# Mixture-of-experts layer in fp32: the further slots' work under the conditional, row additions on VectorE, and the last expert's second product by column halves

## The chip, the cores and the metric

One core of a Trainium2 chip runs the whole program. The time is device microseconds from the start to the end of one execution. The kernel before takes 2110.71 us in the median of three runs (2107.49 to 2116.29).

## The reference

512 tokens of 1024 columns pass two layers. Each layer has a mixer of four branches (sliding-window attention, a recurrent branch, two further attentions), and then a feed-forward block: dense in the first layer, a mixture of eight experts in the second, two experts for each token. Everything is fp32. What the change touches is the end of the second layer:

```python
# D_MODEL 1024, D_FF_EXPERT 1408, 8 experts, top 2 of them for each of 512 tokens
h = silu(x @ exp_w1[e]) * (x @ exp_w3[e])     # [tokens of e, 1408]
y = h @ exp_w2[e]                             # [tokens of e, 1024]
out = layer_norm(DN_ALPHA * x + sum over the token's two experts of weight * y)
```

## The kernel before, in words

**Precision.** A weight piece of 128 x 1024 fp32 comes in by a DMA from SyncE (SP). ScalarE casts it to a rounded 32-bit form (whi, L1152), VectorE subtracts that from the original (wlo, L1153), and TensorE multiplies three times: high by high, high by low, low by high. So each piece costs a ScalarE cast, a VectorE subtraction and twelve or six matmuls in sequence.

**An expert.** Its first 128 tokens are its slots; up to 32 more are its *further* slots. Tokens that chose it are gathered, transposed, and multiplied: `up` does three chunks of columns (512, 512, 384), `turn` transposes the gated product of a chunk (`turn_main` for the 128 slots, the rest of `turn` for the further ones: transposes at L1466, a copy and SiLU on ScalarE at L1471 and L1474, an addition and a product on VectorE at L1472 and L1475), and `down` multiplies by the second matrix, eleven pieces. The order is written out: rows of the next expert are turned and its first chunk is multiplied before this one's `down` begins. A scheduler then sets each engine's order from it; marked lines (`high_priority`) go earlier.

**Further slots.** Their matmuls use the raw fp32 pieces with 32 columns of stationary data, four side by side, and stand under a conditional on the number of tokens of the expert (`further`, L1443): six conditionals in `up` and three in `down`. All engines come past each conditional. In the program before only TensorE has work in them. The buffer po is set to zero by VectorE first (L1404, L1486), so that what comes behind can run whether the block was taken or not: ScalarE copies po to go (L1438) or yo (L1523), and `down_more` adds up four groups by a matmul with a fixed matrix (L1529), VectorE copies (L1531) and GpSimd stores the rows (L1534) to Y in device memory. A token's row in Y is found by its slot number.

**The end.** Rows of experts 0 to 6 are gathered from Y token by token (`ask_rows`, GpSimd's indirect DMA, L1317, two for each block of 128 tokens, eight in all, into four buffers). `take_rows` multiplies each by its weight on ScalarE (L1706) and adds it to x on GpSimd in halves (L1709). The last expert's result isn't stored: `last` splits it, brings it to token order by matmuls with one-hot matrices (L1743 to L1746), adds it to x on VectorE (L1748), and the layer norm follows on VectorE with help of ScalarE and GpSimd.

Of the kernel before, what the change touches and what calls it, by code (L numbers as in the profile page):

```python
# [56 lines left out]
class Net:  # L57
# [1340 lines left out]
    def up(self, e, c, begin=None):  # L1398

        nc, I = self.nc, self.I  # L1400
        mm = nc.tensor.matmul
        n = min(512, FE - c * 512)
        pa, pb, po = self.triple()
        nc.vector.memset(po, 0.0)  # L1404
        r = 32 * (e % 4)
        xh, xl = self.xe[:, e % 2, 0], self.xe[:, e % 2, 1]
        late = []
        for k0 in range(0, KB, 2):
            raws = []
# [29 lines left out]
        return g, go, c, n  # L1439

# [16 lines left out]
    def turn(self, st):  # L1457

        nc = self.nc
        g, go, c, n = st  # L1460
        nb = n // P
        gt, gto = self.gT
        self.turn_main(g, c, n, gt)
        pt = self.ps("y")
# [4 lines left out]
        t = self.rf.tile([P, 4, 64], F32, name="sgo", tag="sgo", bufs=2)[:, 0:nb]  # L1469
        with self.tc.high_priority():  # L1470
            nc.scalar.copy(t, p4[:, :, 0])  # L1471
            nc.vector.tensor_add(t, t, p4[:, :, 1])  # L1472
            s = t[:, :, 0:32]
            nc.scalar.activation(s, s, AF.Silu)  # L1474
            nc.vector.tensor_mul(gto[:, c * 4:c * 4 + nb], s, t[:, :, 32:64])  # L1475

# [3 lines left out]

    def down(self, e, gT):
        nc, I = self.nc, self.I
        mm = nc.tensor.matmul
        gt, gto = gT
        p0, p1, po = self.triple()
        nc.vector.memset(po, 0.0)  # L1486
        late = []
        for f0 in range(0, EB, 2):
            if e == NE - 1 and f0 in (2, 6):
                self.take_rows(f0 // 4 + 1)  # L1490
                self.ask_rows(f0 // 4 + 2)
            fs = range(f0, min(EB, f0 + 2))
            raws = []
            for f in fs:
# [4 lines left out]
                for hf, ps in enumerate((p0, p1)):  # L1499
# [3 lines left out]
                    mm(ps, gt[:, 1, f], a, start=False, stop=f == EB - 1)  # L1503
                raws.append(raw)
            late += list(zip(fs, raws))
# [8 lines left out]
        if e == NE - 1:  # L1514
            self.take_rows(TB - 1)
            return p0, p1, po
        y = self.rf.tile([P, D], F32, name="yr", tag="yr", bufs=2)
        yo = self.rf.tile([P, 512], F32, name="yo", tag="yo", bufs=1)
# [5 lines left out]
        return yo  # L1524

    def down_more(self, e, yo):
# [6 lines left out]
        for hf in range(2):  # L1533
            nc.gpsimd.dma_start(self.Y[r:r + 32, hf * 512:(hf + 1) * 512], ys[32 * hf:32 * hf + 32])  # L1534

    def rest(self, dp):
# [127 lines left out]
    def slots(self):  # L1664
# [25 lines left out]

        z = mp.tile([P, D], F32, name="zero", tag="xg", bufs=2)
        nc.vector.memset(z[0:1], 0.0)
        nc.gpsimd.dma_start(self.Y[(NE - 1) * NS:(NE - 1) * NS + 1, :], z[0:1])

# [7 lines left out]
    def take_rows(self, *tbs):  # L1702
        for tb in tbs:
            for j in range(2):
                rows = self.yg[:, tb % 2 * 2 + j]
                self.nc.scalar.mul(rows, rows, self.wt[:, tb, j:j + 1])  # L1706
                for half in range(2):
                    xs = self.x[tb][half]
                    self.nc.gpsimd.tensor_add(xs, xs, rows[:, half * 512:(half + 1) * 512])  # L1709

    def last_begin(self):

        nc, mp = self.nc, self.rf
        num = self.num_t
        ido = mp.tile([P, 2], F32, name="ido")
        nc.vector.memset(ido, -1.0)
        for h in range(2):
            for i in range(2):
                r = 32 * (2 * i + h)
                nc.vector.tensor_copy(ido[r:r + 32, h:h + 1], self.own[96:128, 9:10])  # L1720
        self.ohl = []
        for n, col in enumerate((self.own[:, NE - 1:NE], ido[:, 0:1], ido[:, 1:2])):
# [4 lines left out]
    def last(self, pss, g, b):  # L1727

        nc, mp = self.nc, self.rf
        mm = nc.tensor.matmul  # L1730
        hl = []
        for n, ps in enumerate(pss):
            t = mp.tile([P, 2, 512], F32R, name="yl", tag="xg" if n == 2 else "yr", bufs=2)
            nc.scalar.copy(t[:, 0], ps)  # L1734
            nc.vector.tensor_sub(t[:, 1], ps, t[:, 0].bitcast(F32))
            hl.append(t)
        tags = ("r", "y", "s", "t", "o", "mm", "mm", "mm")
        for tb in range(TB):
            ts = slice(tb * P, (tb + 1) * P)
            for half in range(2):  # L1740
                ps = self.ps(tags[tb * 2 + half])
                a, o = self.ohl[0][:, ts], self.ohl[1 + half][:, ts]
                mm(ps, a, hl[half][:, 0], start=True, stop=False)  # L1743
                mm(ps, a, hl[half][:, 1], start=False, stop=False)
                mm(ps, o, hl[2][:, 0], start=False, stop=False)
                mm(ps, o, hl[2][:, 1], start=False, stop=True)  # L1746
                xs = self.x[tb][half]
                nc.vector.scalar_tensor_tensor(xs, ps, self.cw[:, tb, NE - 1:NE], xs, op0=OP.mult, op1=OP.add)  # L1748
                self.stats(tb, half)
            self.layer_norm(tb, g, b, spread=True)  # L1750
            self.store_x(tb, self.out)

    def moe(self, dp):
# [9 lines left out]
        self.new_gT()  # L1763
        self.links = {}
        self.preload(PRE)
# [11 lines left out]
        for e in range(NE):  # L1777
            gT = self.gT
            self.turn(st)
            if e > 0:  # L1780
                self.down_more(e - 1, yo)
            if e + 1 < NE:
# [3 lines left out]
            for c in (1, 2):  # L1786
                st = self.up(e, c)
                if c == 1:
                    self.turn(st)
                    self.tokens(e + 2)  # L1790
                    if e == 0:
                        self.dispatch(range(4, 8))
                    if e == 1:
                        self.wt, self.cw = self.weights("")
# [7 lines left out]
            self.turn(last)  # L1802
            if e == NE - 1:
                self.take_rows(0)
                self.ask_rows(1)
                self.last_begin()
            yo = self.down(e, gT)
        self.last(yo, g, b)

# [44 lines left out]
```

## Time and profile before

| | |
|---|---|
| runs | 2110.71 us median (2107.49 to 2116.29) |
| profiled execution | 2107.6 us, span 2105.9 us |
| TensorE (PE) | 96% busy, mean granted clock 0.988 |
| VectorE (DVE) | 65% |
| ScalarE (ACT) | 44% |
| GpSimd (POOL) | 7% (151.1 us) |
| experts of the second layer | from about 1580 us on |

The page gives busy time by engine, the span in slices, the chain that ended last, and groups of instructions by line. Other views of the same trace give windows (busy time of each engine in a stretch), timelines (one engine's instructions in order, with the idle time before them in brackets and what ended it), and waits. Starts are microseconds from the start of the span. `x2` folds two instructions in sequence into one row, whose duration is then that of both.

### The profile page before, as it was taken

The page shows a single profiled execution, that of the slowest core. Times are in us where ns is not written, and L with a number is a line of the kernel's source. Part 1 is how long each engine was busy: PE and PEld are TensorE (multiplying, and loading weights), DVE is VectorE, ACT ScalarE, POOL GpSimd, SP SyncE. Part 2 cuts the span into 40 slices and gives each one's busy share as a digit, 9 for nine tenths or more (in the row PEclk, how much of TensorE's full clock was granted, in tenths as well). Part 3 has the DMA queues.
Part 4 walks back from the last instruction along what each step waited for, and adds up shares of the span by engine and source line. Part 5 has one row for each costly group of instructions (what it writes and reads, how often), then busy time and mean ns, then how long its engine had stood idle before and what let it go on. Part 6 is the DMA issues. An engine that isn't in the chain of part 4 may idle for free. (4 is left out here: it accounts for less than half of the span.)

```text
span 2105.9 us, 31148 instructions
## 1 busy us (share of the span) xinstructions
PE 2019.7 (96%) x11240; PEld 1569.9 (75%) x11240; DVE 1366.6 (65%) x2732; ACT 918.0 (44%) x1561; POOL 151.1 (7%) x211
## 2 busy tenths in 40 slices
PE   8999999999999999999999999999989999999994
PEld 7767777778888888888767778768877766677663
DVE  5677779844563333236676769844568877788778
ACT  3354543333232222113464553332326666677663
POOL 1020200000000000000011200000000000000043
PEclk9999999999999999999999999999999999999997
DMA  5231213343343334233221213313538988898872
GB/s 159 69 84 39 57 41 90 90 125 96 94 146 99 101 93 133 92 98 115 77 58 43 70 41 90 90 51 95 176 128 308 352 291 304 295 342 306 293 280 82
DMA packets 274976, 294.56 MB, mean 140 GB/s; under 512 B 23852, under 2 KB 203416, under 8 KB 274808
## 3 DMA queue, kind: packets, MB, share of 16 engines
q1 hardware_dynamic: 267736, 273.90, 40.2%
q0 software_dynamic: 7072, 18.49, 2.8%
q8 instruction: 97, 1.59, 0.3%
q14 instruction: 71, 0.58, 0.1%
HBM read 276.74 MB, written 15.60 MB: 139 GB/s over the span
## 5 line engine op out<-in xcount | busy, mean ns | idle before, releaser
L98 ACT CAST whi<-wraw 128x1024 fp32r<-128x1024 f32 (+1 forms) x218 | 228.1, 1046 | 625.4 <-PE ps_mm L112 376.9
L99 DVE TENSOR_TENSOR wlo<-wraw,whi 128x1024 fp32r<-128x1024 f32 (+1 forms) x218 | 265.5, 1218 | 361.2 <-ACT whi L98 355.0
L113 PE MATMUL ps_mm<-xh,wlo 128*128 128x512 f32 (+1 forms) x1288 | 494.9, 384 | 3.1 <-DVE rs L259 3.1
L111 PE MATMUL ps_mm<-xh,whi 128*128 128x512 f32 (+1 forms) x1288 | 496.5, 386 | 0.6 <-ACT whi L98 0.5
L112 PE MATMUL ps_mm<-xl,whi 128*128 128x512 f32 (+1 forms) x1288 | 492.1, 382 | 0.3 <-DVE xl L233 0.3
L113 PEld LDWEIGHTS ps_mm<-xh,wlo 128*128 128x128 f32 x1288 | 243.7, 189 | 49.8 <-DVE wlo L99 3.4
L111 PEld LDWEIGHTS ps_mm<-xh,whi 128*128 128x128 f32 x1288 | 243.8, 190 | 46.5 <-issue 2.6
L112 PEld LDWEIGHTS ps_mm<-xl,whi 128*128 128x128 f32 x1288 | 243.7, 189 | 45.8 <-issue 2.3
L1153 DVE TENSOR_TENSOR wlo<-mwraw,whi 128x1024 fp32r<-128x1024 f32 (+1 forms) x98 | 124.2, 1282 | 17.2 <-ACT whi L1152 16.0
L1152 ACT CAST whi<-mwraw 128x1024 fp32r<-128x1024 f32 (+1 forms) x98 | 95.9, 1005 | 16.0 <-PE ps_t L1503 10.1
L470 ACT COPY bt_pt<-ps_t 128x512 f32<-128x512 f32 (+2 forms) x80 | 41.7, 522 | 85.4 <-PE ps_t L467 84.6
L1153 DVE TENSOR_TENSOR mwlo<-mwraw,mwhi 128x1024 fp32r<-128x1024 f32 (+1 forms) x62 | 71.9, 1175 | 6.9 <-ACT mwhi L1152 6.4
L451 ACT ACTIVATE bt_pt<-ps_s,mx 128x256 f32<-128x256 f32 (+3 forms) x128 | 61.8, 487 | 21.8 <-DVE mx L445 18.0
L260 POOL TENSOR_TENSOR rs<-rs,mhalf 128x1 f32<-128x1 f32 x16 | 13.8, 861 | 724.2 <-DVE rs L259 724.2
L442 DVE TENSOR_REDUCE mx<-ps_s 128x2 f32<-128x512 f32 (+3 forms) x80 | 48.5, 607 | 22.1 <-PE ps_s L406 21.1
L1152 ACT CAST mwhi<-mwraw 128x1024 fp32r<-128x1024 f32 (+1 forms) x62 | 61.0, 999 | 3.2 <-DMA mwraw<-in_exp_w_dram 2.3
L1114 DVE TENSOR_TENSOR bt_pt<-bt_pt,ps_mm 128x512 f32<-128x512 f32 x22 | 15.1, 688 | 70.4 <-PE ps_mm L113 63.0
L467 PE MATMUL ps_t<-ident,bt_pt 128*128 128x128 f32 x272 | 51.5, 283 | 6.0 <-DVE bt_pt L461 4.8
L609 DVE MAX8 m<-bt_pt 128x8 f32<-128x256 f32 (+2 forms) x96 | 53.8, 560 | 2.7
L1153 DVE TENSOR_TENSOR wlo<-ring,whi 128x1024 fp32r<-128x1024 f32 (+1 forms) x45 | 51.5, 1160 | 2.5 <-DMA mwraw<-in_exp_w_dram 1.2
L610 DVE MATCH_REPLACE8 bt_pt<-m,bt_pt 128x256 f32<-128x256 f32 (+2 forms) x96 | 52.1, 543 | 0.0
L111 PE MATMUL ps_mm<-bt_o,whi 128*128 128x512 f32 x128 | 51.2, 400 | 0.4 <-ACT bt_o L511 0.4
(710 smaller groups left out, 4119.1 us busy)
## 6 DMA issues: line engine op xcount, KB each, us to landing
mwraw<-in_exp_w_dram SPq DMA_DIRECT2D x124, 512.0 KB
wraw<-in_w_in_dram SPq DMA_DIRECT2D x106, 512.0 KB
wraw<-in_ffn_w_dram SPq DMA_DIRECT2D x66, 512.0 KB
ring<-in_exp_w_dram SPq DMA_DIRECT2D x60, 512.0 KB
wraw<-in_exp_w_dram SPq DMA_DIRECT2D x32, 512.0 KB
mwraw<-in_exp_w_dram SPq DMA_DIRECT2D x36, 384.0 KB
wraw<-in_w_branch_dram SPq DMA_DIRECT2D x20, 512.0 KB
wraw<-in_w_out_dram SPq DMA_DIRECT2D x16, 512.0 KB
```

The costliest lines, as they stand in the source:

```text
L98: nc.scalar.copy(h, src)
L99: (low or nc.vector).tensor_sub(l, src, h.bitcast(F32))
L111: mm(ps, wh, xh, start=start, stop=False)
L112: mm(ps, wh, xl, start=False, stop=False)
L113: mm(ps, wl, xh, start=False, stop=stop)
L442: nc.vector.tensor_reduce(mx[:, 0:nh], s3, op=OP.max, axis=AX.X)
L451: nc.scalar.activation(p3[:, h], s3[:, h], AF.Exp, bias=nm[:, h:h + 1], scale=0.125, accum_out=mx[:, 4 + h:5 + h])
L467: nc.tensor.transpose(pt[:, i * P:(i + 1) * P], p3[:, h, kb * P:(kb + 1) * P], self.ident)
L609: nc.vector.max(m8, sc[:, :nk])
L610: nc.vector.match_replace(sc[:, :nk], m8, sc[:, :nk], REPL)
L1152: self.chain("hi", lambda: nc.scalar.copy(hi[:, :n], src))
L1153: self.chain("lo", lambda: nc.vector.tensor_sub(lo[:, :n], src, hi[:, :n].bitcast(F32)))
```

## The change

Five things are done together.

1. The transposes of the further slots, their ScalarE and VectorE work, the copy of po and the fold of `down` move into the conditionals (`turn_more`, `down_more`). po isn't cleared any more but in the last expert. The first rows of Y for further slots, 225 of them, are set to zero once, while the first expert runs (`empty`: a GpSimd memset and two stores).
2. `take_rows` is 16 fused multiply-adds on VectorE in the place of 8 ScalarE products and 16 GpSimd additions.
3. The last expert's second product runs over the left 512 output columns first and then over the right ones (`down_last`), six pieces each: five of 128 x 1024 that hold two steps of 512 columns, and one of 128 x 512. There are three conditionals in each half.
4. `last` is called for each half. The further slots' sum is one tile for the half, so that four tiles are split, not three; matmuls of the fold are 32 as before.
5. One one-hot matrix serves the further slots, not two.

```diff
@@ up
-        nc.vector.memset(po, 0.0)
...
                 with self.further(e):
+                    if late[0][0] == 0 and c > 0:
+                        self.turn_more(c - 1)
                     for kk, raws in late:
...
+                    if k0 == KB - 2:
+                        go = self.go[c] = self.rf.tile([P, 512], F32, name="go", tag="go", bufs=2)
+                        nc.scalar.copy(go[:, :n], po[:, :n])
...
-            go = self.rf.tile([P, 512], F32, name="go", tag="go", bufs=2)
-            nc.scalar.copy(go[:, :n], po[:, :n])
@@ down
-        nc.vector.memset(po, 0.0)
...
                 with self.further(e):
+                    if late[0][0] == 0:
+                        self.turn_more(2)
                     for f, w in late:
...
+                    if late[-1][0] == EB - 1:
+                        self.down_more(e, po)
...
-            nc.scalar.copy(yo, po)
+    def down_more(self, e, po):
+        nc = self.nc
+        yo = self.rf.tile([P, 512], F32, name="yo", tag="yo", bufs=1)
+        nc.scalar.copy(yo, po)
         ps = self.ps("y")
         nc.tensor.matmul(ps[0:64], self.ident64, yo, start=True, stop=True)
...
+    def down_last(self, g, b):
...
+        for half in range(2):
+            cs = slice(half * 512, half * 512 + 512)
+            ps, po = [self.ps(t) for t in (("s", "t"), ("o", "mm"))[half]]
+            nc.vector.memset(po, 0.0)
+            late = []
+            for f0 in range(0, EB, 2):
+                if half == 0 and f0 in (2, 6, 10):
+                    self.take_rows(f0 // 4 + 1)
+                    if f0 < 10:
+                        self.ask_rows(f0 // 4 + 2)
+                m = min(2, EB - f0)
+                raw = self.moe_raw()[:, :m * 512]
...
+                for i in range(m):
+                    f = f0 + i
+                    wh, wl = h[:, i * 512:(i + 1) * 512], l[:, i * 512:(i + 1) * 512]
+                    self.chain("mm", lambda: mm(ps, gt[:, 0, f], wh, start=f == 0, stop=False))
+                    mm(ps, gt[:, 0, f], wl, start=False, stop=False)
+                    mm(ps, gt[:, 1, f], wh, start=False, stop=f == EB - 1)
+                    late.append((f, raw[:, i * 512:(i + 1) * 512]))
+                if len(late) >= 2 * HOLD or f0 + 2 >= EB:
+                    with self.further(e):
+                        if half == 0 and late[0][0] == 0:
+                            self.turn_more(2)
+                        for f, w in late:
+                            q = 32 * (f % 4)
+                            mm(po[q:q + 32], gto[:, f], w, start=f < 4, stop=f >= EB - 4, skip_group_check=True)
+                    late = []
+            self.last(half, ps, po, g, b)
@@ take_rows
-                self.nc.scalar.mul(rows, rows, self.wt[:, tb, j:j + 1])
                 for half in range(2):
                     xs = self.x[tb][half]
-                    self.nc.gpsimd.tensor_add(xs, xs, rows[:, half * 512:(half + 1) * 512])
+                    self.nc.vector.scalar_tensor_tensor(xs, rows[:, half * 512:(half + 1) * 512],
+                                                        self.wt[:, tb, j:j + 1], xs, op0=OP.mult, op1=OP.add)
```

The instructions' order on two engines shows where the moved work stands now. First TensorE, at the last conditional of `down` of expert 6. `gt` is the transposed product, `gto` that of the further slots, `ring`, `wraw` and `mwraw` are raw pieces, `whi`/`wlo` and `mwhi`/`mwlo` split ones. Before:

```order
L1507 COMPARE_AND_BRANCH
L1511 MATMUL ps_mm<-ring,gto 32x512 x4
L1511 MATMUL ps_mm<-wraw,gto 32x512 x2
L1507 UNCONDITIONAL_BRANCH x2
L1501 MATMUL ps_mm<-mwhi,gt 128x512 x2
L1502 MATMUL ps_mm<-mwlo,gt 128x512
L1503 MATMUL ps_mm<-mwhi,gt 128x512
L1502 MATMUL ps_mm<-mwlo,gt 128x512
L1503 MATMUL ps_mm<-mwhi,gt 128x512
L1501 MATMUL ps_mm<-whi,gt 128x512 x2
L1529 MATMUL ps_y<-yo,ident_110 64x512
L1502 MATMUL ps_mm<-wlo,gt 128x512
```

And of the change:

```order
L1506 COMPARE_AND_BRANCH
L1512 MATMUL ps_mm<-ring,gto 32x512 x4
L1512 MATMUL ps_mm<-wraw,gto 32x512 x2
L1528 MATMUL ps_y<-yo,ident_110 64x512
L1506 UNCONDITIONAL_BRANCH x2
L1501 MATMUL ps_mm<-mwhi,gt 128x512 x2
L1502 MATMUL ps_mm<-mwlo,gt 128x512
L1503 MATMUL ps_mm<-mwhi,gt 128x512
L1502 MATMUL ps_mm<-mwlo,gt 128x512
L1503 MATMUL ps_mm<-mwhi,gt 128x512
L1501 MATMUL ps_mm<-whi,gt 128x512 x2
L1502 MATMUL ps_mm<-wlo,gt 128x512
```

The fold of the further slots (L1529, now L1528) has moved from between the dense matmuls to the end of the block, ahead of them.

The second place is VectorE from the last subtractions to the first folding instruction. Before (`yl` is the last expert's split result, `bt_x` are the rows of x):

```order
L1153 TENSOR_TENSOR mwlo<-wraw,mwhi 128x1024 x2
L1153 TENSOR_TENSOR wlo<-mwraw,whi 128x1024
L1507 REGISTER_ALU x2
L1507 COMPARE_AND_BRANCH
L1507 UNCONDITIONAL_BRANCH x2
L1153 TENSOR_TENSOR wlo<-mwraw,whi 128x1024 x2
L1735 TENSOR_TENSOR yl<-ps_o,yl 128x512
L1735 TENSOR_TENSOR yl<-ps_s,yl 128x512
L1735 TENSOR_TENSOR yl<-ps_t,yl 128x512
L1748 SCALAR_TENSOR_TENSOR bt_x<-ps_r,cw,bt_x 128x512
```

And of the change, from the first product's last conditional to the second's first:

```order
L1751 SCALAR_TENSOR_TENSOR bt_x<-ring,wt,bt_x 128x512
L1153 TENSOR_TENSOR mwlo<-wraw,mwhi 128x1024
L1751 SCALAR_TENSOR_TENSOR bt_x<-ring,wt,bt_x 128x512
L1153 TENSOR_TENSOR wlo<-mwraw,whi 128x1024
L1751 SCALAR_TENSOR_TENSOR bt_x<-ring,wt,bt_x 128x512
L1153 TENSOR_TENSOR wlo<-mwraw,whi 128x1024 x2
L1153 TENSOR_TENSOR mwlo<-mwraw,mwhi 128x512
L1751 SCALAR_TENSOR_TENSOR bt_x<-ring,wt,bt_x 128x512 x9
L1776 TENSOR_TENSOR yl<-ps_s,yl 128x512
L1776 TENSOR_TENSOR yl<-ps_t,yl 128x512
L1543 MEMSET ps_mm 128x512
L1776 TENSOR_TENSOR yl<-ps_o,yl 128x512
```

Three fused additions stand between the last subtractions and nine in a row behind them; the subtractions of the first half's sums come only after those, and behind them the conditionals of the second half and the folds of both halves.

## Rows read from the trace of the kernel before

**Rows 1.** The page's busy table: busy us, share of the span, instructions.
```profile
PE 2019.7 (96%) x11240; PEld 1569.9 (75%) x11240; DVE 1366.6 (65%) x2732; ACT 918.0 (44%) x1561; POOL 151.1 (7%) x211
```

**Rows 2.** Windows: us, busy us by engine, TensorE's clock, DMA share, GB/s.
```profile
1640.00:2020.00 380.00, 374.70 (x1900) 265.63 (x1899) 300.68 (x345) 253.77 (x338) 15.93 (x24) 1.00 0.86 303
...
1842.90:1897.50 54.60, 53.13 (x244) 40.90 (x243) 48.02 (x56) 40.54 (x55) 3.17 (x5) 1.00 0.95 340
...
2034.00:2046.30 12.30, 9.22 (x43) 7.94 (x41) 10.70 (x11) 9.68 (x15) 9.45 (x7) 0.86 1.04 409
...
2058.00:2064.00 6.00, 0.62 (x2) 0.00 (x0) 6.00 (x1) 2.00 (x2) 6.00 (x6) 0.50 0.25 83
```

**Rows 3.** Timelines of the end: start, us, engine, line, [idle before <- releaser].
```profile
2033.70 1.15 ACT L1706 ACTIVATE ring<-ring,wt 128x1024 f32<-128x1024 f32 x1 [2.73 <-DMA ring<-Y,slot_i]
...
2052.25 4.07 DVE L1153 TENSOR_TENSOR wlo<-mwraw,whi 128x1024 fp32r<-128x1024 f32 x1
...
2056.81 9.95 DVE L1153 TENSOR_TENSOR wlo<-mwraw,whi 128x1024 fp32r<-128x1024 f32 x2
...
2057.18 7.37 POOL L1709 TENSOR_TENSOR bt_x<-bt_x,ring 128x512 f32<-128x512 f32 x6
...
2065.69 0.79 PE L1502 MATMUL ps_s<-wlo,gt 128*128 128x512 f32 x1 [7.07 <-DVE wlo L1153]
...
2071.93 1.23 DVE L1153 TENSOR_TENSOR wlo<-mwraw,whi 128x1024 fp32r<-128x1024 f32 x1 [0.62 <-ACT whi L1152]
...
2080.53 0.75 DVE L1748 SCALAR_TENSOR_TENSOR bt_x<-ps_r,cw,bt_x 128x512 f32<-128x512 f32 x1 [0.78 <-PE ps_r L1746]
```

**Rows 4.** Waits in the experts' stretch: waiter <- awaited: us, times, longest.
```profile
ACT go L1438 <- PE ps_o L1429: 20.0, 5, 4.7
...
ACT yo L1523 <- PE ps_mm L1511: 9.3, 3, 5.8
...
PEld ps_mm L1501 <- issue: 6.7, 10, 0.8
...
PEld ps_mm L1502 <- DVE wlo L1153: 5.7, 7, 0.8
```

**Rows 5.** TensorE's timeline at transposes of further slots in a skipped expert (3 and 2 of them).
```profile
1864.10 0.40 PE L1416 MATMUL ps_s<-whi,xe 128*128 128x512 f32 x1
...
1864.90 0.39 PE L1418 MATMUL ps_s<-whi,xe 128*128 128x512 f32 x1
...
1875.26 0.39 PE L1416 MATMUL ps_t<-mwhi,xe 128*128 128x512 f32 x1
1875.49 0.38 PE L1466 MATMUL ps_y<-ident,go 128*128 128x128 f32 x2
...
1875.94 0.39 PE L1418 MATMUL ps_t<-mwhi,xe 128*128 128x512 f32 x1
```

**Rows 6.** TensorE's timeline at the fold of a skipped expert.
```profile
1893.43 0.63 PE L1501 MATMUL ps_mm<-whi,gt 128*128 128x512 f32 x2
1894.00 1.07 PE L1529 MATMUL ps_y<-yo,ident 128*64 128x512 f32 x2
1895.00 0.50 PE L1502 MATMUL ps_mm<-wlo,gt 128*128 128x512 f32 x1
```

**Rows 7.** Timelines of TensorE and ScalarE behind a taken block of expert 6.
```profile
2014.54 0.73 PE L1501 MATMUL ps_mm<-mwhi,gt 128*128 128x512 f32 x2
...
2014.66 0.59 ACT L1523 COPY yo<-ps_mm 128x512 f32<-128x512 f32 x1 [5.82 <-PE ps_mm L1511]
```

**Rows 8.** Single lines: count, ns min/median/max, first and last start; a DMA's landing.
```profile
L274 DVE SCALAR_TENSOR_TENSOR bt_pt<-bt_pt,rs,bt_v x16: 740/746/751, 578.8 to 966.8; 128x512 f32<-128x512 f32 x16
...
L1152 ACT CAST whi<-mwraw x98: 816/1050/1073, 1574.8 to 2070.8; 128x1024 fp32r<-128x1024 f32 x77, 128x768 fp32r<-128x768 f32 x21
...
L1404 DVE MEMSET ps_o<- x15: 485/485/485, 1581.0 to 1992.7; 128x512 f32 x15
...
DMA to landing us min/median/max: 4.9/6.7/8.1
```

More of the change, by code (lines that the diff above doesn't have):

```diff
@@ L1457, in turn, with turn_more @@
     def turn(self, st):
+        g, c, n = st
+        self.turn_main(g, c, n, self.gT[0])
+    def turn_more(self, c):
         nc = self.nc
-        g, go, c, n = st
+        go, gto = self.go[c], self.gT[1]
+        n = min(512, FE - c * 512)
         nb = n // P
-        gt, gto = self.gT
-        self.turn_main(g, c, n, gt)
         pt = self.ps("y")
@@ L1469, in turn @@
         t = self.rf.tile([P, 4, 64], F32, name="sgo", tag="sgo", bufs=2)[:, 0:nb]
[L1470 to L1475, printed above, removed]
+        nc.scalar.copy(t, p4[:, :, 0])
+        nc.vector.tensor_add(t, t, p4[:, :, 1])
+        s = t[:, :, 0:32]
+        nc.scalar.activation(s, s, AF.Silu)
+        nc.vector.tensor_mul(gto[:, c * 4:c * 4 + nb], s, t[:, :, 32:64])
     def new_gT(self):
@@ L1479, in new_gT, with down @@
                    self.rf.tile([P, EB, 32], F32, name="gto"))
-    def down(self, e, gT):
+    def down(self, e):
         nc, I = self.nc, self.I
         mm = nc.tensor.matmul
-        gt, gto = gT
+        gt, gto = self.gT
         p0, p1, po = self.triple()
-        nc.vector.memset(po, 0.0)
         late = []
         for f0 in range(0, EB, 2):
-            if e == NE - 1 and f0 in (2, 6):
-                self.take_rows(f0 // 4 + 1)
-                self.ask_rows(f0 // 4 + 2)
             fs = range(f0, min(EB, f0 + 2))
-            raws = []
             for f in fs:
@@ L1503, in down @@
                     mm(ps, gt[:, 1, f], a, start=False, stop=f == EB - 1)
-                raws.append(raw)
-            late += list(zip(fs, raws))
+                late.append((f, raw))
             if len(late) >= 2 * HOLD or f0 + 2 >= EB:
                 with self.further(e):
+                    if late[0][0] == 0:
+                        self.turn_more(2)
                     for f, w in late:
@@ L1534, in down_more @@
             nc.gpsimd.dma_start(self.Y[r:r + 32, hf * 512:(hf + 1) * 512], ys[32 * hf:32 * hf + 32])
+    def down_last(self, g, b):
+        nc, I, e = self.nc, self.I, NE - 1
+        mm = nc.tensor.matmul
+        gt, gto = self.gT
+        for half in range(2):
[10 more added lines that the diff above has]
+                raw = self.moe_raw()[:, :m * 512]
+                with self.tc.high_priority():
+                    self.chain("load", lambda: nc.sync.dma_start(
+                        raw.rearrange("p (k c) -> p k c", k=m),
+                        I["exp_w2"][0, e, f0 * P:(f0 + m) * P, cs].rearrange("(k p) c -> p k c", p=P)))
+                h, l = self.moe_split(raw)
+                for i in range(m):
[14 more added lines that the diff above has]
+            self.last(half, ps, po, g, b)
     def rest(self, dp):
@@ L1689, in slots, with empty @@
         nc.vector.tensor_copy(self.slot, sf)
-        z = mp.tile([P, D], F32, name="zero", tag="xg", bufs=2)
-        nc.vector.memset(z[0:1], 0.0)
-        nc.gpsimd.dma_start(self.Y[(NE - 1) * NS:(NE - 1) * NS + 1, :], z[0:1])
+    def empty(self):
+        z = self.rf.tile([P, D], F32, name="zero", tag="yr", bufs=2)
+        self.nc.gpsimd.memset(z, 0.0)
+        n = (NE - 1) * (NS - P) + 1
+        for r in range(0, n, P):
+            m = min(P, n - r)
+            self.nc.gpsimd.dma_start(self.Y[(NE - 1) * P + r:(NE - 1) * P + r + m, :], z[0:m])
     def ask_rows(self, *tbs):
@@ L1714, in last_begin @@
         num = self.num_t
[L1715 to L1720, printed above, removed]
+        ido = mp.tile([P, 1], F32, name="ido")
+        for i in range(4):
+            nc.vector.tensor_copy(ido[32 * i:32 * i + 32], self.own[96:128, 9:10])
         self.ohl = []
-        for n, col in enumerate((self.own[:, NE - 1:NE], ido[:, 0:1], ido[:, 1:2])):
+        for n, col in enumerate((self.own[:, NE - 1:NE], ido)):
             t = mp.tile([P, T], F32R, name="ohl", tag="g", bufs=3)
@@ L1725, in last_begin, with last @@
             self.ohl.append(t)
-    def last(self, pss, g, b):
+    def last(self, half, ps, po, g, b):
         nc, mp = self.nc, self.rf
@@ L1731, in last @@
         hl = []
[L1732 to L1735, printed above, removed]
+        for n, src in enumerate((ps, po)):
+            t = mp.tile([P, 2, 512], F32R, name="yl", tag=("yr", "xg")[n], bufs=2)
+            nc.scalar.copy(t[:, 0], src)
+            nc.vector.tensor_sub(t[:, 1], src, t[:, 0].bitcast(F32))
             hl.append(t)
-        tags = ("r", "y", "s", "t", "o", "mm", "mm", "mm")
         for tb in range(TB):
             ts = slice(tb * P, (tb + 1) * P)
[L1740 to L1751, printed above, removed]
+            out = self.ps((("r", "y", "mm", "mm"), ("r", "y", "s", "t"))[half][tb])
+            for n in range(2):
+                for i in range(2):
+                    mm(out, self.ohl[n][:, ts], hl[n][:, i], start=n == 0 and i == 0, stop=n == 1 and i == 1)
+            xs = self.x[tb][half]
+            nc.vector.scalar_tensor_tensor(xs, out, self.cw[:, tb, NE - 1:NE], xs, op0=OP.mult, op1=OP.add)
+            self.stats(tb, half)
+            if half:
+                self.layer_norm(tb, g, b, spread=True)
+                self.store_x(tb, self.out)
     def moe(self, dp):
@@ L1802, in moe @@
             self.turn(last)
-            if e == NE - 1:
+            if e + 1 < NE:
+                self.down(e)
+            else:
                 self.take_rows(0)
@@ L1806, in moe @@
                 self.last_begin()
-            yo = self.down(e, gT)
-        self.last(yo, g, b)
+                self.down_last(g, b)
 def build(tc, I, out, taps=None, stage=99):
```

14 lines of the change are left out of this document (3 added, 11 removed).

## The prediction

> **What bounds the kernel now.** I read the page's busy table first, then the windows of the mixture-of-experts stretch, then the timelines of TensorE, VectorE and GpSimd at the places that the change edits. TensorE is busy 96% of the span [rows 1], and while the experts run it is 374.70 of 380 us, at full clock; VectorE beside it is 300.68 [rows 2]. So in that stretch time is saved by taking work off TensorE, and lost by making TensorE wait. The end is another matter. From 2046 on TensorE waits for VectorE, whose subtractions are stretched, and from 2080.53 VectorE alone does the last layer norm [rows 3]. The profiled run took 2107.6 us, 1.7 more than its span; the median of the three runs is 2110.71, 3.1 above it. I sum against the profiled run and add the 3.1 at the end. Half a per cent, about 10.6 us, is what a measurement of this kernel can tell from no change.
>
> **Skipped experts: the transposes and the fold.** Eight experts, of which the wait of ScalarE for L1511 shows three that take the conditional block (three waits, [rows 4]); five skip it. Today TensorE transposes the further slots of all eight. In a skipped expert one pair of transposes moves the second matmul behind it from an expected 1875.26 + 2 x 0.23 = 1875.72 to 1875.94, so 0.22 us, and the group of three in the last chunk from 1864.56 to 1864.90, 0.34 us [rows 5]. Eleven transposes are four pairs and one three: 4 x 0.22 + 0.34 = 1.2 us. The fold of the further slots (two fp32 passes, L1529) stands between a pair that starts at 1893.43 and a matmul at 1895.00, which would be due at 1893.90 [rows 6]: 1.1 us, in which a wait for VectorE may hide, so 0.6 to 1.1. Experts 0, 2, 4 and 5 save both, 4 x 2.3 = 9.2; the last one, which has no such fold, saves 1.2. Together **10.4 us** (8.4 at the lower price of the fold). The conditionals themselves stay: nine for each expert, at some two thirds of a microsecond of TensorE each (L1501's weight loads idled 6.7 us at ten of them with no other wait, [rows 4]); the last expert's three new ones fall where TensorE waits for VectorE anyway.
>
> **Taken experts: a new wait.** The fold now stands inside the conditional, behind the last small matmul and ahead of the dense ones (first order piece of the change). Before, TensorE went on with dense matmuls at 2014.54 while ScalarE copied yo from 2014.66 for 0.59 us [rows 7]. Now TensorE must sit through that copy, about 0.75 us with the handover, and VectorE copies ys before it leaves. Behind ScalarE in its queue stand the casts of the next weight pieces, and behind VectorE their subtractions; TensorE has one split piece in hand, six matmuls of 0.23 us and two more that need only the cast, 1.9 us, against a cast and a subtraction that end about as late. So about 1.0 us at this block. The three transposing blocks of such an expert send ScalarE and VectorE into the block with TensorE too, but there 16 small matmuls follow the transposes and cover the copy and the product; I take 0.4 for the three together. Three experts: 3 x 1.4 = **4.2 us lost**, from 2.3 (the yo copy alone) upwards; the upper end is the slower rival below.
>
> **Relief of VectorE.** The memsets of 0.485 us, 15 of them in one row of L1404 [rows 8] and 32 in all, shrink to two, and the small additions and products of skipped experts go. TensorE's weight loads waited 5.7 us in seven waits for a subtraction at L1502 alone [rows 4], but all of TensorE's idle time from 1640 to 2020 is 380 - 374.70 = 5.3 us [rows 2]. So the gain lies between 0 and 5; as most of that idle time stands at conditionals I take **1.5**.
>
> **The last expert and the row additions.** Beside GpSimd's six additions (7.37 us), two subtractions took 9.95 us, where an undisturbed one takes 1.23, and one before them 4.07 [rows 3]. That is 7.5 + 2.8 = 10.3 us, and TensorE waited 7.07 for it. It wasn't the loads: from 2058 to 2064 the DMA engines were busy a quarter of the time [rows 2]. With the additions off GpSimd these 10.3 us go. The Trainium skill, SBUF — State Buffer, "Who interferes with whom", says that a VectorE instruction with two inputs in SBUF and a GpSimd instruction that reads SBUF exclude each other for a whole instruction. By that rule too all of the stretch goes, and a fused addition beside a gather, which only writes, should stay at its own price; the trace has no such pair to confirm it.
>
> What comes instead: 16 fused multiply-adds on VectorE. The layer norm's instruction of this kind and shape takes 0.746 us [rows 8]; so 11.8 us in all, 12 of them in this stretch. In the order three stand ahead of the last weight subtractions (2.2 us) with one memset (0.5). The last subtraction thus ends 10.3 - 2.7 = 7.6 us earlier, if no load or gather stops it. Behind it stood 2080.53 - 2073.16 = 7.4 us to the first folding instruction [rows 3]. Now nine fused additions (6.7), three subtractions of the sums at about 0.7 and the second memset stand there, 9.3 us, beside which TensorE does the second half's 33 matmuls (7.7 us, hidden). The eighth gather can only be issued when an earlier addition among the nine has freed its buffer, and lands 4.9 to 8.1 us later, median 6.7 [rows 8]; some five of the nine don't need it, so VectorE waits about 2. That makes 11.3, 3.9 more than before. Net **3.7 us gained**; between 7.6 - 1.9 = 5.7 with no wait for gathers, and 7.6 - (9.3 + 6.7 - 7.4) - 2 = -3.0 where the eighth is waited for in full and earlier ones hold VectorE for 2 more. The folds and layer norm behind keep their 22 us on VectorE: all eight folds of both halves stand behind the last conditionals. At the start, ScalarE's wait of 2.73 us for the first gather [rows 3] becomes one of VectorE, with subtractions behind it; the gather starts earlier, since the further rows are stored sooner. I put that at nothing, within 1.5 either way.
>
> **Sum.** 10.4 - 4.2 + 1.5 + 3.7 = 11.4 us. 2107.6 - 11.4 = 2096.2, and in the frame of the median 2099.3: I say 2099.
>
> **Rivals.**
> - More is gained (2092): taken blocks cost only the yo copy (2.3), VectorE's relief is the full 5, the tail gives 5.7: 10.4 - 2.3 + 5 + 5.7 = 18.8. For it: VectorE loses four memsets and more of its 48.02 us in a skipped expert [rows 2], and TensorE's waits for subtractions shrink with it. Against: TensorE's idle time is small. Chance 0.19.
> - The meetings at the taken blocks cost half a split (2108). There are four in an expert, three transposing and one folding, twelve in all. Already ScalarE waited 20.0 us in five of its copies of go [rows 4], with casts queued behind. At 1.1 us each, half of a cast and a subtraction, 13.2 us go: 10.4 + 1.5 + 3.7 - 13.2 = 2.4 gained. Chance 0.20.
> - Slower (2130): the same meetings, with nothing split in hand when the block ends, so that TensorE waits through a copy, a cast and a subtraction, 0.59 + 1.05 + 1.23 = 2.87 us [rows 3, 7, 8], twelve times: 34.4, against gains of 15.6. It decides from 2.2 us a meeting. Against it: TensorE had a split piece and more in hand in the one block that I followed. Chance 0.12.
> - The loads bound the skipped experts 4 and 5 (2104). In the stretch of expert 4 the DMA engines are busy 0.95 of the time, at 340 GB/s [rows 2]. If they can't be hurried, its and its neighbour's 4.6 us are lost. An expert's weights are 17.3 MB (three matrices of 1024 x 1408 in fp32), so 52.3 us instead of 54.6 wants 331 GB/s; and 409 GB/s were moved later on [rows 2]. Chance 0.08. The Trainium skill, SBUF — State Buffer, "Summary: rules for kernel authors", gives about 358 GB/s for loads from device memory; the 409 of this trace is above it, and even by the page an expert's loads need an estimated 48.3 us, which leaves the forecast alone.
>
> **Chances and range.** The forecast has 0.41, by itself 2092 to 2105; a little over two thirds of it, 0.29, lies below 2100.2, where faster by over half a per cent begins. With the first rival, faster has 0.48; same has 0.12 + 0.20 + 0.08 = 0.40; slower 0.12. The range runs from 2088, which leaves out some 0.07 of the first rival, to 2113, which takes in the second and leaves out the slower one.
>
> **What would show it.** In the changed profile: no transposes of go and no L1529-like fold in five experts, whose stretch (54.6 us for expert 4) falls by some 2.3; in the three taken ones TensorE idle before the fold for ScalarE's copy, some 0.8 us, and little before the next subtraction. Subtractions after 2040 all at about 1.23 us; the fused additions at 0.74, nine of them in a row with one wait of about 2 us for a gather; the first folding instruction some 4 us earlier against the start of the last product. I am wrong if TensorE waits over 2 us behind taken blocks, if skipped experts don't shorten, or if the gathers hold the last subtractions back.

## The result: slower, and where the time went

The changed kernel takes 2129.37 us in the median of five runs (2122.65 to 2129.98), against 2110.71 us (five runs by then, 2104.15 to 2116.29); the ratio is 1.0083, with an interval of 1.0055 to 1.0111. The forecast was 2099, faster; the time lies above its range and at the number of the slower rival, 2130. The profiled execution took 2122.65 us, the lowest of the five, 15 us above the one of before.

The start of TensorE's last dense matmul of `down` marks the end of each expert in its timeline. These are the windows of the changed kernel from the end of expert 0 to that of expert 1, and so on to expert 6; then to the first folding instruction, and to the end (columns as in [rows 2]):

```profile
1652.66:1723.79 71.13, 67.69 (x354) 44.16 (x353) 46.35 (x51) 40.14 (x54) 2.59 (x5) 1.00 0.78 267
1723.79:1783.02 59.23, 56.28 (x267) 41.00 (x266) 44.40 (x45) 38.13 (x48) 2.60 (x4) 1.00 0.89 314
1783.02:1853.61 70.59, 67.10 (x352) 43.92 (x351) 46.34 (x51) 40.15 (x55) 2.60 (x5) 1.00 0.78 269
1853.61:1908.03 54.42, 51.95 (x231) 39.74 (x229) 43.62 (x44) 37.13 (x46) 1.33 (x2) 1.00 0.93 328
1908.03:1966.95 58.92, 55.98 (x262) 40.58 (x261) 43.71 (x44) 37.60 (x47) 0.54 (x1) 1.00 0.87 301
1966.95:2036.82 69.87, 66.19 (x343) 43.03 (x342) 45.45 (x50) 39.08 (x53) 1.56 (x3) 1.00 0.70 245
2036.82:2091.93 55.11, 42.63 (x178) 32.22 (x176) 45.46 (x56) 28.02 (x35) 12.14 (x9) 0.93 0.70 250
2091.93:2120.90 28.97, 8.21 (x25) 6.25 (x25) 23.16 (x43) 6.55 (x9) 7.98 (x7) 0.62 0.19 73
```

The same windows of the kernel before:

```profile
1651.56:1717.25 65.69, 65.39 (x357) 44.38 (x355) 49.02 (x56) 41.90 (x57) 3.18 (x5) 1.00 0.87 308
1717.25:1775.69 58.44, 57.23 (x280) 42.25 (x278) 48.54 (x56) 40.76 (x55) 3.76 (x5) 1.00 0.89 320
1775.69:1841.21 65.52, 65.06 (x351) 43.84 (x350) 48.52 (x55) 40.56 (x55) 2.64 (x4) 1.00 0.84 287
1841.21:1895.80 54.59, 53.12 (x243) 40.89 (x242) 48.01 (x55) 40.53 (x55) 3.15 (x4) 1.00 0.94 337
1895.80:1953.75 57.95, 56.76 (x276) 41.83 (x274) 48.04 (x55) 40.73 (x55) 1.63 (x3) 1.00 0.88 310
1953.75:2018.41 64.66, 64.29 (x348) 43.49 (x347) 47.73 (x54) 39.95 (x54) 1.57 (x3) 1.00 0.73 255
2018.41:2080.50 62.09, 46.60 (x187) 34.92 (x186) 50.68 (x43) 37.06 (x47) 35.65 (x27) 0.86 0.59 223
2080.50:2105.90 25.40, 5.66 (x25) 4.30 (x23) 21.33 (x41) 6.07 (x8) 7.00 (x7) 0.71 0.22 83
```

Read the first number of each row. The taken experts 1, 3 and 6 are 5.4, 5.1 and 5.2 us longer; the skipped ones 2, 4 and 5 are +0.8, -0.2 and +1.0. Together 384.16 - 366.85 = 17.3 us are lost by the end of expert 6. From there on 84.1 us stand against 87.5, a gain of 3.4. Expert 0 ends 1.1 us later. The order of the program puts the first chunk of the next expert ahead of this one's `down`, so the windows of experts 2 and 5 hold the first two taken blocks of experts 3 and 6; only expert 4's window holds no taken block.

Read then TensorE's busy time: in a skipped expert it did fall, by 0.8 to 1.2 us, but in expert 4 its idle time rose from 54.59 - 53.12 = 1.5 to 54.42 - 51.95 = 2.5. In a taken one, busy time rose by 1.9 to 2.3 us, and idle time from 0.4 to 3.7 in expert 6. Why busy time rises there, with about as many matmuls, was not tried. VectorE and ScalarE have less to do in each of the six experts. So the engines that were relieved are the ones that TensorE now waits for:

```profile
PE ps_y L1528 <- ACT yo L1526: 2.1, 3, 0.7
PE ps_s L1415 <- ACT mwhi L1152: 1.8, 4, 0.5
PE ps_mm L1416 <- DVE wlo L1153: 1.7, 3, 0.6
PE ps_t L1416 <- DVE mwlo L1153: 1.5, 2, 0.8
PE ps_r L1452 <- DVE g L1440: 1.4, 3, 0.5
PE ps_s L1415 <- ACT whi L1152: 1.4, 3, 0.5
PE ps_s L1416 <- DVE wlo L1153: 1.1, 3, 0.4
PE ps_s L1415 <- ACTq L1423: 0.9, 2, 0.4
```

These are TensorE's waits from 1652 to 2036 (waiter, awaited, us, times, longest). The kernel before has 0.2 us in each of four rows there, all for its own queue. Only the first row is the wait that I had priced. Five of the others, 7.5 us together, are casts and subtractions that come too late; one is a product on VectorE (g), and one is ScalarE's queue at a conditional.

How they come to be late, in a taken expert: the timelines of TensorE, ScalarE and VectorE at the last block of expert 6's second chunk, in the changed kernel.

```profile
1979.74 1.04 PE L1430 MATMUL ps_o<-ring,xo 128*32 128x512 f32 x8
1982.46 0.49 PE L1415 MATMUL ps_t<-mwhi,xe 128*128 128x512 f32 x1
1983.19 0.44 PE L1415 MATMUL ps_mm<-mwhi,xe 128*128 128x384 f32 x1 [0.24 <-ACT mwhi L1152]
1983.72 0.50 PE L1416 MATMUL ps_t<-mwlo,xe 128*128 128x512 f32 x1
...
1980.87 0.59 ACT L1434 COPY go<-ps_o 128x512 f32<-128x512 f32 x1 [5.02 <-PE ps_o L1430]
1981.36 1.05 ACT L1152 CAST mwhi<-ring 128x1024 fp32r<-128x1024 f32 x1
...
1982.44 1.23 DVE L1153 TENSOR_TENSOR mwlo<-ring,mwhi 128x1024 fp32r<-128x1024 f32 x1 [4.78 <-ACT mwhi L1152]
```

ScalarE stands 5.02 us at the copy to go, inside the block, until TensorE has done the small matmuls. Only then comes the cast of the chunk's last piece, and VectorE, which stood 4.78 us for that cast, subtracts until 1983.67; TensorE, which could have begun the low half at 1982.7, starts it at 1983.72, with a single matmul of the next chunk between. Before, ScalarE waited for the same matmuls (3.09 us at 1967.02), but with the last cast already made: in its order there the cast of this piece stood ahead of the copy, and the copy stood behind the block:

```profile
1962.88 1.04 ACT L1152 CAST mwhi<-ring 128x1024 fp32r<-128x1024 f32 x1
1967.02 0.59 ACT L1438 COPY go<-ps_o 128x512 f32<-128x512 f32 x1 [3.09 <-PE ps_o L1429]
```

In a skipped expert there is no product to wait for, and yet the order stays. ScalarE's timeline at the end of expert 4's third chunk, and TensorE's beside it, in the changed kernel:

```profile
1875.43 0.49 ACT L1439 ACTIVATE g<-ps_mm 128x384 f32<-128x384 f32 x1 [2.17 <-PE ps_mm L1417]
1875.82 1.04 ACT L1152 CAST whi<-mwraw 128x1024 fp32r<-128x1024 f32 x1
...
1876.10 0.34 PE L1417 MATMUL ps_mm<-whi,xe 128*128 128x384 f32 x1
1876.91 0.50 PE L1415 MATMUL ps_s<-whi,xe 128*128 128x512 f32 x1 [0.47 <-ACT whi L1152]
```

And the kernel before at the same place:

```profile
1861.22 0.48 ACT L1438 COPY go<-ps_mm 128x384 f32<-128x384 f32 x1 [0.94 <-PEq L1424]
1861.60 1.05 ACT L1152 CAST whi<-mwraw 128x1024 fp32r<-128x1024 f32 x1
1863.43 0.49 ACT L1435 ACTIVATE g<-ps_mm 128x384 f32<-128x384 f32 x1 [0.78 <-PE ps_mm L1418]
```

Before, the next chunk's first cast is made between the copy to go and the SiLU of g. Now it stands behind the SiLU, which waits 2.17 us for the sum that it reads, almost to the end of TensorE's chunk: the cast starts when TensorE needs it, and TensorE waits 0.47 us.

The fold's block of expert 6 is as I had described it (TensorE, ScalarE, VectorE of the changed kernel):

```profile
2031.33 1.03 PE L1512 MATMUL ps_mm<-wraw,gto 128*32 128x512 f32 x4
2033.04 1.07 PE L1528 MATMUL ps_y<-yo,ident 128*64 128x512 f32 x2 [0.69 <-ACT yo L1526]
2034.04 0.73 PE L1501 MATMUL ps_mm<-mwhi,gt 128*128 128x512 f32 x2
...
2032.40 0.59 ACT L1526 COPY yo<-ps_mm 128x512 f32<-128x512 f32 x1 [6.87 <-PE ps_mm L1512]
...
2034.15 0.68 DVE L1530 COPY ys<-ps_y 64x512 f32<-64x512 f32 x1 [6.61 <-PE ps_y L1528]
```

TensorE waits 0.69 us, and goes on at once behind it. But ScalarE and VectorE have stood 6.87 and 6.61 us with nothing prepared meanwhile, and in the next chunk TensorE waits for them:

```profile
2039.64 0.50 PE L1416 MATMUL ps_t<-wlo,xe 128*128 128x512 f32 x1 [0.76 <-DVE wlo L1153]
```

### The profile page after: what moved, and what is told of

Its sections match the earlier page's. It is cut to its first block, busy times and chain, and to the rows that moved or that the text cites. A ratio compares the mean times of both kernels' runs of the same rounds, so it can differ in the third digit from the quotient of the medians.

```text
span 2120.9 us, 31008 instructions
## 1 busy us (share of the span) xinstructions
PE 2021.4 (95%) x11177; PEld 1560.1 (74%) x11177; DVE 1338.8 (63%) x2683; ACT 894.4 (42%) x1506; POOL 126.4 (6%) x189
## 5 line engine op out<-in xcount | busy, mean ns | idle before, releaser
L1153 DVE TENSOR_TENSOR wlo<-mwraw,whi 128x1024 fp32r<-128x1024 f32 (+2 forms) x98 | 111.0, 1157 | 17.5 <-ACT whi L1152 16.4
L1152 ACT CAST whi<-mwraw 128x1024 fp32r<-128x1024 f32 (+2 forms) x98 | 94.6, 1000 | 9.3 <-DMA mwraw<-in_exp_w_dram 7.4
L1153 DVE TENSOR_TENSOR mwlo<-mwraw,mwhi 128x1024 fp32r<-128x1024 f32 (+2 forms) x63 | 71.1, 1148 | 22.8 <-ACT mwhi L1152 22.1
L470 ACT COPY bt_pt<-ps_t 128x512 f32<-128x512 f32 (+2 forms) x80 | 41.8, 523 | 85.1 <-PE ps_t L467 84.3
L1152 ACT CAST mwhi<-mwraw 128x1024 fp32r<-128x1024 f32 (+2 forms) x63 | 60.8, 992 | 5.3 <-PE ps_t L1417 1.9
```

Of the source, the lines that this page charges most:

```text
L1152: self.chain("hi", lambda: nc.scalar.copy(hi[:, :n], src))
L1153: self.chain("lo", lambda: nc.vector.tensor_sub(lo[:, :n], src, hi[:, :n].bitcast(F32)))
```

## The experiments

The theory was: all the loss is in the conditionals, because ScalarE and VectorE have to meet TensorE there. The rival: the end of the kernel got slower. In the results "experts 1 to 6" is the time between the ends of experts 0 and 6 (366.85 before, 384.16 after), and "the rest" what follows to the end of the span (87.5 and 84.1). They are read from one profile of each kernel. The six profiles of kernels whose conditionals are those of before (with e1_tail, e3_rows, e4_halves, e11_rows5 and e12_halves5) agree in experts 1 to 6 to 0.3 us, 366.7 to 367.0; the rest is less steady, 83.9 and 82.0 in two profiles of one kernel (e4_halves, e12_halves5).

**e1_tail** puts `up`, `turn`, `down` and `down_more` of the kernel before into the changed one:

```diff
-                    if late[0][0] == 0 and c > 0:
-                        self.turn_more(c - 1)
...
+            nc.scalar.copy(go[:, :n], po[:, :n])
```

> The changed kernel with its conditionals as in the kernel before: transposes, copies and fold of the further slots stand outside again; the fused row additions on VectorE and the last product by halves stay. Theory (the work inside the conditionals costs all of the loss, since ScalarE and VectorE must wait there for TensorE): the end of expert 6 comes within 2 us of the kernel before, the time is 2 to 4 us under the kernel before, some 2105 to 2109. Rival (the end is what got slower): the end of expert 6 as before, but a time of 2115 or more.

Measured: ratio 1.0016 (0.9997 to 1.0035). Experts 1 to 6 take 366.8 us, as before to 0.3 us in each, so taking the conditionals' work out takes the loss out. But the end took 90.1 us, 2.6 more than before, and the median of 2116.88 us is over the theory's 2105 to 2109 and where the rival had put it.

**e2_ifs** is the other half: the kernel before with `turn_more` and `down_more` inside, and its own end.

> The kernel before with only the work of the further slots moved into the conditionals; row additions on ScalarE and GpSimd and the last product as before. Theory (conditionals cost all): experts 1, 3 and 6 each 5 us longer than before, skipped ones within 1 us of before, some 17 us at the end of expert 6, time 2124 to 2132. Rival (the end is what got slower): under 2112.

Measured: 1.0082 (1.0055 to 1.0109), which is the changed kernel's whole loss. Experts 1 to 6 take 384.5 us; taken ones 71.2, 70.7 and 69.8, skipped ones 59.3, 54.5 and 59.0. The conditionals' work alone makes the loss, and the rival falls as its cause. The rest takes 85.1 us here, by the end of the kernel before.

**e3_rows** and **e4_halves** part the end.

```diff
@@ e3_rows, against before
-                self.nc.scalar.mul(rows, rows, self.wt[:, tb, j:j + 1])
...
+                    self.nc.vector.scalar_tensor_tensor(xs, rows[:, half * 512:(half + 1) * 512],
+                                                        self.wt[:, tb, j:j + 1], xs, op0=OP.mult, op1=OP.add)
@@ e4_halves, against e1_tail: take_rows of before
+                self.nc.scalar.mul(rows, rows, self.wt[:, tb, j:j + 1])
...
+                    self.nc.gpsimd.tensor_add(xs, xs, rows[:, half * 512:(half + 1) * 512])
```

> The kernel before with only the row additions on VectorE; last product not halved. If GpSimd's reads stretch VectorE's subtractions, none of them takes over 1.3 us (8.8 before) and TensorE's wait of 7 us goes; 16 fused additions of 0.74 us come in, net 0 to 6 us faster than the kernel before. If the stretch has another cause, subtractions of over 3 us remain.

> The kernel of e1 with the row additions on ScalarE and GpSimd as before; so the last product by halves alone. If the row additions make the gain of the end, this one is slower than e1 by 3 to 10 us and shows subtractions of over 3 us beside GpSimd's additions; if the halves make it, it is as fast as e1.

VectorE's subtractions of the end for one of the split tiles (count, ns min/median/max), in the kernel before:

```profile
L1153 DVE TENSOR_TENSOR wlo<-mwraw,whi x8: 945/1212/8818, 2044.0 to 2071.9; 128x1024 fp32r<-128x1024 f32 x7, 128x768 fp32r<-128x768 f32 x1
```

with additions on VectorE (e3_rows):

```profile
L1153 DVE TENSOR_TENSOR wlo<-mwraw,whi x11: 953/1218/1225, 2043.3 to 2075.4; 128x1024 fp32r<-128x1024 f32 x7, 128x768 fp32r<-128x768 f32 x4
```

and on GpSimd (e4_halves):

```profile
L1153 DVE TENSOR_TENSOR wlo<-mwraw,whi x11: 682/1214/2322, 2040.2 to 2075.6; 128x1024 fp32r<-128x1024 f32 x6, 128x768 fp32r<-128x768 f32 x4, 128x512 fp32r<-128x512 f32 x1
```

With the additions off GpSimd no subtraction of the end takes over 1.23 us; with them on it, they take up to 2.3, and 8.8 in the kernel before. From 2020 us on, all seven subtractions of the kernel before that took over 1.3 us ran beside a GpSimd addition, and the 17 that ran beside none took at most 1.21. So GpSimd's additions are the cause of the stretch [rows 3]; that it is what they read isn't parted here. It goes the other way too: in e4_halves one addition took 4.23 us, with three undisturbed subtractions beside it, where others take 1.25 to 1.3. Yet the second expectation fails in both its cases: e4_halves, with a stretch up to 2.3 us, was faster than e1_tail (the rest took 83.9 us against 90.1) and about level with e3_rows (83.2). Neither has more than its one profiled execution here; both were timed below.

**e5_before_skip** and **e6_after_skip** let no expert in, so that no engine can wait inside a block. Both leave out the further slots' products:

```diff
-        return self.tc.If(((self.more >> e) & 1) > 0)
+        return self.tc.If(((self.more >> e) & 1) > 1)
```

> The kernel before with a condition that no expert meets: the further slots' products are left out for all experts. It is the base for the next run. Experts 1, 3 and 6 should fall from 65 to about 55 to 58 us, as the skipped ones take.

> The changed kernel with the same condition that no expert meets: no block is entered, so no engine waits inside one; the order of the instructions and the conditionals stay. If the loss is only made by waits inside the blocks, each expert is 1 to 2.3 us shorter than in the run with the kernel before (the transposes and the fold are skipped eight times). If the order of ScalarE's casts around the conditionals eats the saving, experts are within 1 us of it and TensorE shows new waits for a cast at the start of chunks.

Measured: experts 1 to 6 take 327.6 us by the kernel before and 327.2 by the changed one. The skipped transposes and folds, 2.3 us an expert by my sum, bring 0.4 us in six, though no block is entered. At the start of the next expert's first chunk TensorE waits as in the changed kernel; its row, and the two largest rows of TensorE's waits in experts 1 to 6 (e6_after_skip):

```profile
1949.21 0.51 PE L1415 MATMUL ps_s<-whi,xe 128*128 128x512 f32 x1 [0.47 <-ACT whi L1152]
...
PE ps_s L1415 <- ACT whi L1152: 2.8, 6, 0.5
PE ps_s L1415 <- ACTq L1423: 2.2, 5, 0.5
```

TensorE's busy time over the six experts falls by 7.1 us, from 318.9 to 311.8; the waits listed come to 7.0 us, and the same view of e5_before_skip lists none. So skipped experts lose by the order of ScalarE's and VectorE's work, and not by waits in blocks: the wait for that cast is the largest share, the queue of ScalarE at the conditionals the next.

**e7_go_out** takes only the copy to go out of the blocks again, and **e8_fold_out** only the fold. Each clears po again for what it takes out, and e8_fold_out also drops the zeroing of Y's rows (`empty`), which runs in expert 0:

```diff
@@ e7_go_out
+        nc.vector.memset(po, 0.0)
...
-                    if k0 == KB - 2:
-                        go = self.go[c] = self.rf.tile([P, 512], F32, name="go", tag="go", bufs=2)
-                        nc.scalar.copy(go[:, :n], po[:, :n])
...
+            go = self.go[c] = self.rf.tile([P, 512], F32, name="go", tag="go", bufs=2)
+            nc.scalar.copy(go[:, :n], po[:, :n])
@@ e8_fold_out
-                    if late[-1][0] == EB - 1:
-                        self.down_more(e, po)
```

> The changed kernel with the copy of po to go outside the conditionals, and its memset back; transposes, SiLU and fold stay inside. If the copy of go in the block is what costs (ScalarE's next cast stands behind it), taken experts fall from +5.3 to about +3 us against before, and the third chunk loses its +0.8 in all experts. If the transposing and folding blocks cost it, taken experts stay at +4.5 or more.

> The changed kernel with the fold of the further slots and the copy to yo outside, as before; transposes and the copy to go stay inside. If the fold's block costs 1.0 us in a taken expert, taken experts fall from +5.3 to about +4.3 us, and skipped ones rise by about 1.1 for the fold. If it costs most, taken experts fall to +2.

Measured for e7_go_out: taken experts 68.0, 67.7 and 67.5 (+2.2 to +2.8 against before, not +5.2), skipped ones 57.0, 53.5 and 56.8 (1.1 to 1.4 *under* before). Experts 1 to 6 take 370.3: of the 17.3 us, this one copy's place gives back 13.8. ScalarE at the place shown above has the cast ahead of the SiLU again, and TensorE goes on without a gap:

```profile
1873.27 1.05 ACT L1152 CAST whi<-mwraw 128x1024 fp32r<-128x1024 f32 x1
1874.96 0.49 ACT L1437 ACTIVATE g<-ps_mm 128x384 f32<-128x384 f32 x1 [0.63 <-PE ps_mm L1418]
...
1875.63 0.33 PE L1418 MATMUL ps_mm<-whi,xe 128*128 128x384 f32 x1
1875.81 0.39 PE L1416 MATMUL ps_s<-whi,xe 128*128 128x512 f32 x1
```

Whether it is the copy in the block or the order in which the scheduler then puts the casts isn't parted: no run has the copy inside and the casts as before.

For e8_fold_out: taken experts 68.7, 68.3 and 68.3, so the fold's block cost 1.6 to 2.4 us and not 1.0; skipped ones 59.0, 55.3 and 59.7, at most 0.8 us more for the fold. 5.0 us come back in all.

**e9_go_in** does this one thing alone in the kernel before; VectorE clears go in po's place.

> The kernel before with one thing alone: ScalarE's copy of po to go moves into the last block of each chunk, and VectorE clears go in the place of po. If that copy's place is the larger part of the loss, taken experts are some 3 us longer than before (68 to 69) and skipped ones 1 us longer (59.4, 55.6, 59), 10 to 15 us at the end of expert 6. If it costs only beside the other work in the blocks, experts stay within 1 us of before.

Measured: experts 1 to 6 take 375.5, 8.7 us more than before; taken ones +0.3, +3.1 and +2.7, skipped ones +0.9, +0.5 and +1.2. So the copy's place alone, with the clearing that goes with it, costs half of the loss, under the 10 to 15 that I expected; beside the other work in the blocks it costs more. Of expert 1's loss 1.1 us lies behind its mark, where its fold stands in this run; why the rest is so small I don't know.

**e10_both_out** leaves only the transposing blocks: copy to go and fold outside, po cleared again, and no `empty`.

> The changed kernel with the copy to go and the fold outside the conditionals, and only transposes, SiLU and product of the further slots inside; fused additions and halves stay. By the sum of e7 and e8 taken experts are within 0.5 us of before and skipped ones 0.3 under it; with the end as in the changed kernel 3 us are gained, ratio 0.998. If the transposing block costs by itself, taken experts stay 2 us longer, ratio 1.001.

Measured: 1.0016 (1.0005 to 1.0027). Taken experts +0.7, +0.5 and +1.4 against before, skipped ones -0.4, -0.6 and -0.6: 368.0 us for experts 1 to 6, 1.1 over before. So the transposing block itself is in the main paid for by what skipped experts save. The time came out as in the second case, but for another reason: the rest took 86.9, so the end gave next to nothing.

**e11_rows5** and **e12_halves5** are e3_rows and e4_halves again, each timed in twelve executions.

> The kernel of e3 (the kernel before with only the row additions on VectorE), timed. Its one profile had 4 us less than before from expert 0 on: ratio 0.997 to 0.999. If that was chance, 1.000.

> The kernel of e4 (the kernel before with only the last product by halves), timed. Its one profile had 3.5 us less than before from expert 0 on: ratio 0.997 to 0.999. If that was chance, 1.000.

Measured: 0.9974 (0.9964 to 0.9985) and 0.9970 (0.9954 to 0.9985). Each part of the new end alone beats the kernel before by 5 to 6 us (and the changed one by more); the rest took 83.2 and 82.0 us in their profiles. The two together (e1_tail) don't add, they cancel. In e1_tail's trace VectorE stands 8.38 us for the first gather, does seven fused additions ahead of the last pieces' subtractions, and then waits 3.76 us for a cast. TensorE waits 6.80 us there for the subtraction behind the first gather, and 2.29 and 1.88 us for two casts, which themselves wait for loads; in the changed kernel it waits 3.14 us behind the first gather, and for no cast. What of this undoes the gain was not tried.

## Why the prediction was wrong, step by step

- **Skipped experts, 10.4 us to be saved: wrong, and the first step that failed.** TensorE's busy time fell by 0.8 to 1.2 us in each, half of the 2.3 or less, and idle time took all of it: expert 4, whose window has no taken block, was 0.2 us shorter, and experts 2, 4 and 5 together took 1.6 us longer. I costed the removal at TensorE's own time, and of what could be late next I named only the loads. With no block entered, e6_after_skip saved 0.4 us in six experts; with the copy to go outside (e7_go_out), 1.1 to 1.4 us came in each.
- **Taken experts, 4.2 us to be lost: right in sign, 15.7 us in size.** I priced the fold's block at 1.0 and the three transposing ones at 0.4. The fold's block is worth 1.6 to 2.4 (e8_fold_out). The copy to go in the last block of each chunk had no price in my sum at all, though the diff shows it: it is the largest part, 13.8 us of 17.3 with the skipped experts (e7_go_out), 8.7 alone (e9_go_in). The parts don't add: 13.8 and 5.0 exceed the 16.2 that both give back in e10_both_out.
- **Relief of VectorE, 1.5 us: none to be seen.** VectorE's busy time fell by 2.2 to 4.4 us in an expert, and TensorE waits for it longer. Its share of busy time wasn't the limit there; how far its order runs ahead of TensorE was.
- **The end, 3.7 us gained: 3.4 in the profile, near by luck.** The stretched subtractions went, and the fused additions took 0.743 to 0.753 us, also beside gathers. The Trainium skill (SBUF — State Buffer, "Who interferes with whom") says that a VectorE instruction with two inputs in SBUF contends with a GpSimd instruction that reads SBUF, not with one that only writes it; the trace agrees, if a gather only writes, as I had assumed. The wait for a late gather among the nine was 1.05 us, where I had said 2; the nine fused additions stood as seven and two, as VectorE's timeline of the changed kernel shows, with TensorE's wait behind the first of the sixteen:

```profile
2048.82 0.75 DVE L1751 SCALAR_TENSOR_TENSOR bt_x<-ring,wt,bt_x 128x512 f32<-128x512 f32 x1 [4.37 <-DMA ring<-Y,slot_i]
...
2082.41 4.72 DVE L1751 SCALAR_TENSOR_TENSOR bt_x<-ring,wt,bt_x 128x512 f32<-128x512 f32 x7
2088.18 1.42 DVE L1751 SCALAR_TENSOR_TENSOR bt_x<-ring,wt,bt_x 128x512 f32<-128x512 f32 x2 [1.05 <-DMA ring<-Y,slot_i]
...
2050.76 0.80 PE L1416 MATMUL ps_s<-wlo,xe 128*128 128x512 f32 x1 [3.14 <-DVE wlo L1153]
```

  The first folding instruction came 55.1 us after the end of expert 6, not 62.1: 7.0 earlier, where I had said 3.7. But from there to the end took 29.0 us against 25.4, a part that I had kept as before; the second half's sums are split among the folds there. Every profile with halves has 27.6 to 30.4 us in this part, every one without has 25.3 to 25.4. So two errors cancel. The first gather, which I had put at nothing within 1.5, cost TensorE 3.14 us, since a subtraction stands behind the fused addition that waits for it. And the size is fragile: the same end took 82.7 us in e8_fold_out, 83.7 in e7_go_out, 84.1 in the changed kernel, 86.9 in e10_both_out and 90.1 in e1_tail, and TensorE's wait behind the first gather rises in the same order, 1.83, 3.13, 3.14, 5.87 and 6.80 us. With the old end, e2_ifs took 85.1, so not all of the 3.4 is the new end's. (Sixteen additions at 0.746 are 11.9 us, not 11.8; no term of the sum hangs on it.)
- **The slower rival, chance 0.12:** its place was right, its price not. It wanted 2.87 us at each of twelve meetings, 34.4 us, against gains of 15.6. The trace has 15.7 us in the taken experts, 1.3 at a meeting, and of the gains of 15.6 that it set against them, only the end's came. It hit the time by two errors that cancel.
- **The second rival, half a split at each meeting, chance 0.20:** the nearest in price, 1.1 us at each of twelve meetings where 1.3 was measured. It missed the time because it kept the 10.4 and 1.5 us that didn't come.
- **The loads as a bound:** the skipped experts didn't shorten, as this rival had it, but TensorE's new waits are for casts and subtractions; and e7_go_out's expert 4 took 53.5 us under the same loads. So they don't bound the 54.4 us of the changed kernel; whether they would allow 52.3 isn't shown.

## What to carry to other kernels

Work moved into a conditional was paid here on every engine that takes part, also where the block is skipped: on the engines that feed the bottleneck, instructions that prepare later pieces came later in the order. So before such a move, compare how many prepared pieces stand ahead of each block in the feeder's order, and treat one piece less as a wait at the consumer; here it came to 1.3 us a meeting, where a whole cast and subtraction are 2.28. Saving time on the bound engine was worth almost nothing here while its feeders ran only one piece ahead. Keeping the one small copy that gates them outside, and paying for clearing its source, gave back 13.8 of 17.3 us.

## What was not expected of the hardware

- Code that all versions share, up to the end of expert 0's first chunk, took from 1590.7 to 1601.1 us in the 14 profiles, with mean granted clocks of 0.982 to 0.989. Parts of a few microseconds are therefore compared from the end of expert 0 on.
- Leaving out the products of the further slots and letting every expert skip took 39 us off experts 1 to 6 of the kernel before (366.85 to 327.6): 10.8 to 11.1 in each taken expert, and 3.3 in experts 2 and 5, whose windows hold the first chunk of a taken one. Each then took 53.9 to 55.1 us, a little under the 55 to 58 expected.
